# Both projections of an MLP on one core: 2x2 blocks with seven products in place of eight

## The chip, the cores and the metric

The kernel runs on one core of a Trainium2 chip. The metric is the device time of one execution in microseconds (us), lower is better. Three runs of the kernel before took 1946.54, 1942.43 and 1945.25 us (median 1945.25).

## What is computed

One inference step of a hybrid decoder layer: an input projection, dilated attention and a state-space branch, an output projection, and then the part that this change touches, a squared-ReLU MLP and the final norm. The prompt has 1024 tokens (1024 features each), the sample 8 tokens, and there are 4096 hidden features. All is float32.

```python
mix = jnp.concatenate([rms_norm(attn) * g_attn, y], axis=-1) @ w_out
x = x + g1 * mix
u = jnp.square(jax.nn.relu(modulate(x, sh2, sc2) @ w_up))     # (1024+8, 1024) @ (1024, 4096)
x = x + g2 * (u @ w_down)                                     # (1024+8, 4096) @ (4096, 1024)
y_prompt = rms_norm(xp) * g_final
```

## The kernel before, in words

Activations lie with the features on the 128 partitions and the tokens along the columns: `x1` is 8 blocks of 128 features by T = 1032 columns (1024 prompt, 8 sample), held in SBUF. A float32 product is made of three matmuls of the rounded type fp32r (`mm3`, L60 to L64): high part by high part, weight high by data low, weight low by data high. The high part is a copy on ACT (L51, for weights L442), the low part a subtract on DVE (L52, for weights L443). A matmul takes a 128x128 block of weights and one of the three column chunks of `NCH`: 352, 352 and 328 columns.

`phase_out` (L1479) is the output projection: 8 feature blocks by 3 chunks, each with 8 blocks of y and 8 of the attention. `gated` (L1402) adds a result, times its gate, into `x1` on DVE (L1406). Behind the groups of a chunk, `h2_stats` and `h2_cols` make the normed and modulated input of the MLP as a pair of tiles (high, low). The last chunk's runs on into the MLP.

`phase_mlp` (L1684) goes through 16 blocks of 256 hidden features: `up_block` of b+1, then `down_block` of b. An up group (one of 6 per block) is 8 k x 3 matmuls into a PSUM bank, then ReLU on ACT (L1723), square on DVE (L1724) and the split of the result (L51, L52). A down group (one of 24 per block) is 2 k x 3 matmuls and one `gated`. The weights come through `WStream`: raw loads of 1 MB, one ahead, split in pieces of 512 columns by `ws.step()`. Each `ws.get` issues two background copies (`background`, L54), which move the sample's key and value caches from DRAM to DRAM: 64 pieces of 512 rows, 2 MB each, all in the MLP.

Every one of these DMAs is issued by SP, in program order. Each engine executes its instructions in program order. `Side` is a generator that is advanced by estimated costs, so that norm work is written between the matmul groups. In the tail the last two blocks are taken in four column ranges, with the final norm of a finished range (`final_tiles`, L1773) beside the matmuls of the next.

Of the kernel before, what the change touches and what calls it, by code (L numbers as in the profile page):

```python
# [14 lines left out]
D = 1024  # L15
S = 1024
NB = 8
T = S + NB
KT = 8
NCH = ((0, 352), (352, 704), (704, 1032))  # L20
EPS = 1e-6
# [6 lines left out]
class Trunk:  # L28
# [364 lines left out]
    def mod_sample(self, pool, x, rb, blk, hi, lo):  # L393
# [5 lines left out]
        self.split(hi, lo, ts)  # L399
class WStream:  # L400
# [113 lines left out]
class InProj:  # L514
# [167 lines left out]
    def feat_gemm(self, acc, wt, col, consume):  # L682
        hi, lo = wt
        for a, b in NCH:
# [7 lines left out]
            consume(a, b, ps[:, :b - a])  # L692
            self.cw.step()
# [225 lines left out]
class Sample:  # L919
# [124 lines left out]
    def decode_scores(self, sb, sc, unit):  # L1044
# [3 lines left out]
        kv = lambda: sb.tile([128, D], F32, name="dkv", tag="dkv", bufs=6)  # L1048
# [352 lines left out]
class Rest:  # L1401
# [11 lines left out]
    def out_group(self, acc, w, x, m, n):  # L1413

        a, b = NCH[n]
# [3 lines left out]
        for k in range(KT):  # L1419
            self.mm3(ps[:, :W], whi[:, k], wlo[:, k], hi[:, k, :W], lo[:, k, :W], k == 0, k == KT - 1)  # L1420
            if k < KT - 1:
                yield 430
        self.gated(m, a, b, ps[:, :W], 2)
        yield 430

    def pair(self, n, c):

        a, b = NCH[n]
# [3 lines left out]
    def y_load(self):  # L1432

        i = self.y_n
        if i < self.y_end:
            self.y_n += 1
            a, e = NCH[i // 4][0], min(NCH[i // 4][1], S)
            k = 2 * (i % 4)
            yt = self.yt_pool.tile([128, 2, 352], F32, name="yt", tag="yt")
# [3 lines left out]
    def y_cols(self, n, cost):  # L1443

        a, b = NCH[n]
# [33 lines left out]
    def phase_out(self, eh, eo, ey, o_tok):  # L1479
# [4 lines left out]
        self.y_end, self.yt_pool = 12, self.pool(ey, "yt", bufs=4, side="right")  # L1484
        for _ in range(4):
            self.y_load()
# [8 lines left out]
        ys, aas, hs = self.ys, [], []  # L1495
        self.h2 = hs
# [23 lines left out]
        def attn_cols(n):  # L1520

            a, b = NCH[n]
# [20 lines left out]
        def h2_stats(sq, p, wait=5000):  # L1543

            yield wait
            for i in range(3):
                nc.tensor.matmul(p[:, i:i + 1], sq[:, 128 * i:128 * i + 128], self.ones[:, 0:1], start=True, stop=True)
            rs = self.sm.tile([128, 3], F32, name="r2", tag="r2", bufs=2)
            self.rstd(self.sm, rs, p[:, 0:3], [128, 3], "r2")
            yield 2500  # L1550
            for i in range(3):
                nc.tensor.transpose(p[:, 128 + 128 * i:256 + 128 * i], rs[:, i:i + 1].to_broadcast([128, 128]), self.ident)
            yield 500

        def h2_cols(n, p, cost=900):

            a, b = NCH[n]
            e, W = min(b, S), b - a
            r = p[:, 128:128 + W]
            hi, lo = pair(n, "h")  # L1560
            hs.append((hi, lo))
            if b > S:
                self.mod_sample(self.sm, self.x1[:, :, S:T], r[:, e - a:W], 3, hi[:, :, e - a:W], lo[:, :, e - a:W])
            ts = {}
            for k in range(KT + 1):
                if k < KT:
                    t = ts[k] = self.sm.tile([128, 352], F32, name="t2", tag="t2", bufs=3)
                    nc.vector.scalar_tensor_tensor(t[:, :e - a], self.x1[:, k, a:e], self.mod[:, 4, k, 0:1], r[:, :e - a],
                                                   op0=OP.mult, op1=OP.mult)
                    nc.scalar.activation(hi[:, k, :e - a], t[:, :e - a], AF.Identity, bias=self.mod[:, 3, k, 0:1], scale=1.0)  # L1570
                if k:
                    nc.vector.scalar_tensor_tensor(lo[:, k - 1, :e - a], ts[k - 1][:, :e - a], self.mod[:, 3, k - 1, 0:1],
                                                   f32(hi[:, k - 1, :e - a]), op0=OP.add, op1=OP.subtract)
                yield cost

        def first_w(wp):

            hi, lo = [self.up.tile([128, 2064], F32R, name="w0", tag="u", bufs=4)[:, 0:2048] for _ in range(2)]
            self.w0 = [t.rearrange("p (k n) -> p k n", k=KT) for t in (hi, lo)]
            raws = []  # L1580
            for i in range(2):
                raw = wp.tile([128, KT, 128], F32, name="ow_raw", tag="ow_raw", bufs=2).rearrange("p k n -> p (k n)")
# [481 lines left out]
```

## Time and profile before

| | |
|---|---|
| median of three runs | 1945.25 us |
| the profiled execution's own time | 1945.86 us |
| its span | 1944.1 us |
| mean granted clock of TensorE over the span | 0.987 |
| busy: PE, PEld, DVE, ACT, POOL | 1865.6, 1737.2, 1176.7, 670.5, 398.8 us |
| DMA: bytes, mean rate | 341.62 MB, 176 GB/s |
| MLP without tail and last part: 1198 to 1905 us | PE busy 706.03 of 707 us |

PE is the TensorE matmul, PEld its weight load, DVE the vector engine, ACT the scalar engine, POOL GpSimd, SP the engine that issues DMAs. A matmul's own duration in the records (0.32 us) overlaps the next one's, so the rate is read from the distance between starts. A DMA share over 1.00 is an overlap of the records likewise. The stretches that are named below are counted in us from the start of the span: input projections 165 to 520, attention and state-space work to about 950, output projection to 1198, MLP to 1944.

### The profile page before, as it was taken

The page shows a single profiled execution, that of the slowest core. Times are in us where ns is not written, and L with a number is a line of the kernel's source. Part 1 is how long each engine was busy: PE and PEld are TensorE (multiplying, and loading weights), DVE is VectorE, ACT ScalarE, POOL GpSimd, SP SyncE. Part 2 cuts the span into 40 slices and gives each one's busy share as a digit, 9 for nine tenths or more (in the row PEclk, how much of TensorE's full clock was granted, in tenths as well). Part 3 has the DMA queues.
Part 4 walks back from the last instruction along what each step waited for, and adds up shares of the span by engine and source line. Part 5 has one row for each costly group of instructions (what it writes and reads, how often), then busy time and mean ns, then how long its engine had stood idle before and what let it go on. Part 6 is the DMA issues. An engine that isn't in the chain of part 4 may idle for free.

```text
span 1944.1 us, 33819 instructions
## 1 busy us (share of the span) xinstructions
PE 1865.6 (96%) x13390; PEld 1737.2 (89%) x13390; DVE 1176.7 (61%) x2886; ACT 670.5 (34%) x1665; POOL 398.8 (21%) x382
## 2 busy tenths in 40 slices
PE   5899999999999989999899999999999999999998
PEld 3679999999999987766677899999999999999997
DVE  4613684857486796888834537655555555555566
ACT  3511434343521324877630324322222222222222
POOL 0011142434230462899400021000000000000000
PEclk8999999999999999999999999999999999999999
DMA  9673212132243766877365113656676656666665
GB/s 283 254 254 127 78 55 65 59 90 85 72 133 129 203 197 172 234 195 195 101 212 195 55 44 109 217 217 217 234 264 237 239 217 216 231 251 250 241 229 174
DMA packets 185546, 341.62 MB, mean 176 GB/s; under 512 B 27296, under 2 KB 152864, under 8 KB 180993
## 3 DMA queue, kind: packets, MB, share of 16 engines
q1 hardware_dynamic: 181804, 326.09, 50.8%
q0 software_dynamic: 3376, 13.30, 2.2%
q8 instruction: 105, 1.72, 0.4%
q14 instruction: 53, 0.43, 0.1%
q10 hardware_dynamic: 208, 0.07, 0.0%
HBM read 304.86 MB, written 168.85 MB: 244 GB/s over the span
## 4 chain that ended last, share of the span: by engine, by line
PE 78%; DVE 7%; POOL 5%; DMA 4%; ACT 2%; issue 2%; SPq 0%; DVEq 0%; POOLq 0%; ACTq 0%
PE acc L62 23%; PE acc L63 22%; PE acc L64 22%; POOL dkv L1082 2%; DMA aw<-in_w_ada 2%; POOL dkv L1086 1%; DVE ab L628 1%; PE y_ps L839 1%; PE y_ps L832 1%; DMA vw_raw<-in_w_in 1%; PE misc L1155 1%; DVE qw_lo L443 1%; PE s L1265 1%; PE o L1303 1%; PE pt L1287 1%
## 5 line engine op out<-in xcount | busy, mean ns | idle before, releaser
L1406 DVE SCALAR_TENSOR_TENSOR x<-acc,mod,x 128x352 f32<-128x352 f32 (+2 forms) x432 | 239.0, 561 | 148.3 <-PE acc L64 142.0
L62 PE MATMUL acc<-u,mw_hi 128*128 128x352 f32 (+3 forms) x800 | 251.7, 315 | 0.2 <-DVE gs L1410 0.2
L63 PE MATMUL acc<-u,mw_hi 128*128 128x352 f32 (+3 forms) x800 | 251.1, 314 | 0.0
L64 PE MATMUL acc<-u,mw_lo 128*128 128x352 f32 (+3 forms) x800 | 250.4, 313 | 0.0
L63 PE MATMUL acc<-h_lo,mw_hi 128*128 128x352 f32 (+1 forms) x720 | 230.3, 320 | 0.0
L62 PE MATMUL acc<-h_hi,mw_hi 128*128 128x352 f32 (+1 forms) x720 | 229.8, 319 | 0.0
L64 PE MATMUL acc<-h_hi,mw_lo 128*128 128x352 f32 (+1 forms) x720 | 229.6, 319 | 0.0
L62 PE MATMUL acc<-h_hi,cw_hi 128*128 128x352 f32 (+1 forms) x576 | 192.5, 334 | 1.1 <-ACT cw_hi L442 1.1
L63 PE MATMUL acc<-h_lo,cw_hi 128*128 128x352 f32 (+1 forms) x576 | 184.5, 320 | 0.0
L64 PE MATMUL acc<-h_hi,cw_lo 128*128 128x352 f32 (+1 forms) x576 | 184.2, 320 | 0.2 <-DVE cw_lo L443 0.2
L1723 ACT ACTIVATE ur<-acc 128x352 f32<-128x352 f32 (+1 forms) x96 | 43.9, 457 | 394.6 <-PE acc L64 394.5
L1724 DVE TENSOR_TENSOR ur<-ur 128x352 f32<-128x352 f32 (+1 forms) x96 | 49.6, 517 | 168.9 <-ACT ur L1723 168.9
L62 PEld LDWEIGHTS acc<-u,mw_hi 128*128 128x128 f32 x800 | 150.4, 188 | 0.9 <-PE acc L64 0.4
L64 PEld LDWEIGHTS acc<-u,mw_lo 128*128 128x128 f32 x800 | 150.6, 188 | 0.0
L62 PE MATMUL acc<-h_hi,qw_hi 128*128 128x256 f32 (+1 forms) x512 | 150.4, 294 | 0.0
L63 PEld LDWEIGHTS acc<-u,mw_hi 128*128 128x128 f32 x800 | 150.3, 188 | 0.0
L64 PE MATMUL acc<-h_hi,qw_lo 128*128 128x256 f32 (+1 forms) x512 | 145.7, 285 | 2.0 <-DVE qw_lo L443 2.0
L63 PE MATMUL acc<-h_lo,qw_hi 128*128 128x256 f32 (+1 forms) x512 | 145.9, 285 | 0.0
L63 PEld LDWEIGHTS acc<-h_lo,mw_hi 128*128 128x128 f32 x720 | 135.4, 188 | 0.0
L62 PEld LDWEIGHTS acc<-h_hi,mw_hi 128*128 128x128 f32 x720 | 135.3, 188 | 0.0
L64 PEld LDWEIGHTS acc<-h_hi,mw_lo 128*128 128x128 f32 x720 | 135.2, 188 | 0.0
L1280 ACT ACTIVATE P<-P,st 128x256 f32<-128x256 f32 (+1 forms) x256 | 118.4, 467 | 2.6 <-DVE st L1269 2.6
(424 smaller groups left out, 4343.0 us busy)
## 6 DMA issues: line engine op xcount, KB each, us to landing
aw<-in_w_ada SPq DMA_DIRECT2D x16, 1024.0 KB
mw_raw<-in_w_down SPq DMA_DIRECT2D x16, 1024.0 KB
out_k_win_sample<-in_cache_k_win SPq DMA_DIRECT2D x8, 2044.0 KB
out_v_win_sample<-in_cache_v_win SPq DMA_DIRECT2D x8, 2044.0 KB
mw_raw<-in_w_up SPq DMA_DIRECT2D x15, 1024.0 KB
cw_raw<-in_w_in SPq DMA_DIRECT2D x24, 512.0 KB
dkv<-in_cache_k_win SPq DMA_DIRECT2D x24, 512.0 KB
dkv<-in_cache_v_win SPq DMA_DIRECT2D x24, 512.0 KB
```

The costliest lines, as they stand in the source:

```text
L62: mm(ps, lhi, rhi, start=first, stop=False)
L63: mm(ps, lhi, rlo, start=False, stop=False)
L64: mm(ps, llo, rhi, start=False, stop=last)
L443: self.pend = lambda: self.K.nc.vector.tensor_tensor(lo, src, f32(hi), op=OP.subtract)
L628: nc.vector.tensor_tensor(r[:, 1, :W], r[:, 1, :W], ab[1][:, 0, :W], op=OP.add)
L832: nc.tensor.matmul(y[64 * a:64 * a + 64, 128 * j:128 * j + 128], xdt[:, h], G[:, h], start=True, stop=(c == 0))
L839: nc.tensor.matmul(y[:, 256:512], Bt, xw.rearrange("p h d -> p (h d)"), start=True, stop=True)
L1082: nc.gpsimd.tensor_tensor(pd, pd, qbs[b], op=OP.mult)
L1280: nc.scalar.activation(P, P, AF.Exp, bias=st[:, i + u, a, 0:1], scale=-1.0, accum_out=st[:, i + u, a, 1:2])
L1406: nc.vector.scalar_tensor_tensor(self.x1[:, m, a:e], ps[:, :e - a], self.mod[:, blk, m, 0:1], self.x1[:, m, a:e], op0=OP.mult, op1=OP.add)
L1723: nc.scalar.activation(r[:, :W], ps[:, :W], AF.Relu)
L1724: nc.vector.tensor_tensor(r[:, :W], r[:, :W], r[:, :W], op=OP.mult)
```

## The change

Matrices are cut in 2x2 blocks and multiplied with seven block products (Strassen's scheme in Winograd's form); the sums of blocks before and after the products are made on DVE and POOL.

- Up: 16 pairs (q) of 128-feature blocks; the 1024 inputs are halved, the 1024 prompt columns too. Seven products per pair (j = 0 to 6), each 4 k x 3 matmuls of 512 columns into one bank. The right operands ("hops") are made once: j = 0, 1 from the normed first half, j = 2 to 6 by `t_prep` with 8 DVE subtracts, 20 splits and 8 POOL subtracts. The weight operands are made for each pair: four POOL subtracts or adds, then a copy on ACT and a subtract on DVE (`split_op`) for each product, written at k = 1 of the product before it.
- What a product gives is combined by `evict` with the earlier ones; ReLU and square are both on ACT. Four more POOL instructions per pair make sums of the squared blocks for the down projection. Seven blocks of 256 KB per pair go to DRAM (`u_d`, 28 MB in all) and come back in the down stage.
- Down: pairs in four chunks (4, 4, 4 and 3 pairs); per chunk and j four feature blocks m, each n k x 3 matmuls of 512 columns. Per m one `step` is written: two DRAM loads, one weight operand, one split of a loaded block. Results of j = 1, 4, 6 are gated into `x1`, those of j = 0, 2, 5, 3 are summed over chunks. In the last chunk the sums are combined by a list (`later`) of 16 gates on DVE and 16 adds on POOL, five entries per m. The last pair is done plainly, in four ranges of 256 columns, with the final norm.
- Sample: its 8 columns go through separate matmuls, in up 16 of 128 columns per pair, in down 4 of 256 columns for each of 32 feature blocks, both with unsplit float32.
- Output projection: chunks of 512, 256 and 264 columns. `x1` is stored to DRAM (24 stores) and reloaded in the down stage; the normed columns of the second half are written over it.
- Background copies: 256 pieces of 128 rows; 72 of them are now issued in the input projections, 184 in the MLP. Fewer buffers: the decode's `dkv` 5 (was 6), `yt` 3 (was 4).

Matmuls of the MLP before: 768 groups of three chunks, 16 x 6 x 24 + 16 x 24 x 6 = 4608 in all. Now 16 x 7 x 12 = 1344 of 512 columns in up, 3 x 7 x 48 + 7 x 36 = 1260 in down, 192 of 256 columns for the last pair, and 384 small ones for the sample.

```diff
+OCH = ((0, 512), (512, 768), (768, 1032))
...
             consume(a, b, ps[:, :b - a])
+            self.background()
...
+        for q in range(16):                                    # up_prep
+            if q < 15:
+                load(q + 1)
...
+            self.sample_up(q, r1, r2)
+            s3 = self.S3.tile()
+            if q >= self.EARLY:
+                op((q, 0), a11)
+            g(s3, a11, a21, op=OP.subtract)
+            g(a11, a22, s3, op=OP.subtract)
+            if q >= self.EARLY:
+                yield (q, 0)
+                op((q, 1), a12)
+            g(a12, a12, a11, op=OP.subtract)
+            g(a21, a21, a22, op=OP.add)
+            if q >= self.EARLY:
+                yield (q, 1)
+            for j, a in ((2, a11), (3, a21), (4, a12), (5, s3), (6, a22)):
+                yield op((q, j), a)
...
+        for k in range(4):                                     # t_prep
+            v(b11[k], b12[k], b11[k], op=OP.subtract)
+            t2.append(self.UB.tile())
+            v(t2[k], b22[k], b11[k], op=OP.subtract)
+            self.split(*hops[2][k], t2[k])
+            yield
...
+            elif j == 4:                                       # evict, up
+                b = st[12, q] = self.UB.tile()
+                v(b, ps, st["t", q], op=OP.add)
+                square(b)
+                b11 = st.pop((11, q))
+                if q < 15:
+                    t1 = st["t1", q] = self.UB.tile()
+                    self.later += [lambda: g(t1, b, b11, op=OP.subtract), store(0, q, b11), store(3, q, t1)]
...
+                def hook(k):                                   # phase_up
+                    if k == 1:
+                        step()
+                        next(side, None)
+                    if k in (0, 2):
+                        self.pop_later(1 + len(self.later) // 8)
+                    if q == 0:
+                        next(side, None)
+
+                product(q, j, bank(), self.ops.pop((q, j)), hook)
+                if j:
+                    self.background()
...
+            if j == 5 and c == len(self.CHUNKS) - 1:           # evict, down
+                add = lambda o, a, b: lambda: nc.gpsimd.tensor_tensor(o[:, m], a[:, m], b[:, m], op=OP.add)
+                self.later += [lambda: gate(m, h0, P0[:, m]), add(U, U, P0),
+                               lambda: nc.sync.dma_start(P0[:, m], self.x1_d[:, m + 4, h1]),
+                               add(V3, V3, U), add(U, U, V5), lambda: gate(m, h1, V3[:, m]), add(V3, V3, V5),
+                               lambda: gate(m + 4, h0, U[:, m]), lambda: gate(m + 4, h1, V3[:, m])]
...
+                        if b == n:                             # phase_down
+                            if m < n or c + 1 < len(self.CHUNKS) and n < 4:
+                                step()
+                            evict(c, j, m, pss[m])
+                            self.pop_later(5)
+                            self.background()
...
-                for a in range(0, 2047, 512):
-                    e = min(a + 512, 2047)
+                for a in range(0, 2047, 128):
+                    e = min(a + 128, 2047)
```

Three places in the engines' order. The first is DVE at the start of the up stage. Before, three kinds of row alternate (square, low part of the result, low part of a weight):

```order
L1724 TENSOR_TENSOR ur<-ur 128x352
L52 TENSOR_TENSOR u<-ur,u 128x352
L443 TENSOR_TENSOR mw_lo<-mw_raw,mw_hi 128x512
```

Now, behind the norm of the last columns (`L1598`), the right operands of `t_prep` stand there (`L1883`, `L1885`, and `tl` from `L53`); `ol<-mr,oh` is the low part of a weight operand, `L1936` the first sum of two products:

```order
L1598 SCALAR_TENSOR_TENSOR t_13196<-x_10902,mod,misc 128x256
L1883 TENSOR_TENSOR x_10902<-x_10902 128x512
L1885 TENSOR_TENSOR ub<-x_10902 128x512
L53 TENSOR_TENSOR tl_13213<-ub,th_13212 128x512
...
L53 TENSOR_TENSOR tl_13215<-x_10902,th_13214 128x512 x4
L1936 TENSOR_TENSOR b_13272<-acc,p_13249 128x512
L53 TENSOR_TENSOR tl_13217<-x_10902,th_13216 128x512 x4
L53 TENSOR_TENSOR ol<-mr,oh 128x512
L53 TENSOR_TENSOR tl_13219<-x_10902,th_13218 128x512 x4
L1936 TENSOR_TENSOR b_13332<-acc,p_13301 128x512
L53 TENSOR_TENSOR ol<-mr,oh 128x512
```

The three rows `L1883`, `L1885`, `L53` come four times. So 8 subtracts and 12 splits stand ahead of the first `ol` shown, which the product (3, 1) needs, and four splits more ahead of the second, for (0, 2).

The second is ACT in the middle of the up stage. Before, each group has three rows:

```order
L1723 ACTIVATE ur<-acc 128x352
L51 CAST u<-ur 128x352
L442 CAST mw_hi<-mw_raw 128x512
```

Now one pair of feature blocks reads (`L1933` evicts the product j = 0, `L1923` is ReLU, `L1924` square, `L52` the high part of the weight operand of the product after next):

```order
L1933 COPY p_14364<-acc 128x512
L52 CAST oh<-mr 128x512
L1923 ACTIVATE ub<-ub 128x512
L1924 ACTIVATE ub<-ub 128x512
L52 CAST oh<-mr 128x512 x2
L52 CAST oh<-ms 128x512
L1923 ACTIVATE ub<-ub 128x512
L1924 ACTIVATE ub<-ub 128x512
L52 CAST oh<-mr 128x512
```

In the products that are squared, the high part of the weight operand of the product after next now stands behind ReLU and square of this one.

The third is DVE in the last chunk of the down stage. Now (`L2161` sums over chunks, `L2150` is a gate; U_16250, U_16251 and U_16252 are the summed products, `ol` and `bo` the low parts of weight and data):

```order
L2161 TENSOR_TENSOR U_16252<-acc,U_16252 128x512
L2150 SCALAR_TENSOR_TENSOR x_16256<-U_16250,mod,x_16256 128x512
L2150 SCALAR_TENSOR_TENSOR x_16256<-U_16251,mod,x_16256 128x512
L2150 SCALAR_TENSOR_TENSOR x_16256<-x_16256,mod 128x512
L53 TENSOR_TENSOR ol<-mr,oh 128x512
L53 TENSOR_TENSOR bo<-ub,bo 128x512
L2150 SCALAR_TENSOR_TENSOR x_16256<-acc,mod,x_16256 128x512
```

and POOL has there, four times over:

```order
L2163 TENSOR_TENSOR U_16250<-U_16250,x_16256 128x512
L2163 TENSOR_TENSOR U_16251<-U_16251,U_16250 128x512
L2163 TENSOR_TENSOR U_16250<-U_16250,U_16252 128x512
L2163 TENSOR_TENSOR U_16251<-U_16251,U_16252 128x512
```

Before, DVE had only `L1406` and `L443` at such a place, and POOL had nothing. Now three of four gates stand behind adds of POOL and ahead of the low parts of the next product.

## Rows read from the trace of the kernel before

**Rows 1.** Windows: input projections, two MLP stretches, tail.
```profile
core 0: us, PE busy (x) PEld busy (x) DVE busy (x) ACT busy (x) POOL busy (x), PEclk, DMA share, GB/s
...
165.00:520.00 355.00, 348.16 (x2431) 335.13 (x2429) 220.51 (x470) 141.75 (x261) 108.88 (x112) 1.00 0.25 70
...
1198.00:1905.00 707.00, 706.03 (x4535) 704.77 (x4533) 417.14 (x980) 167.26 (x340) 1.28 (x1) 1.00 0.65 236
1905.00:1944.00 39.00, 29.97 (x254) 29.38 (x254) 24.17 (x62) 10.14 (x32) 0.00 (x0) 0.94 0.37 136
```

**Rows 2.** Timeline of PE: start us, us, instruction; 352, 328 and 256 columns.
```profile
1215.63 0.31 PE L62 MATMUL acc<-h_hi,w 128*128 128x328 f32 x1
...
1219.23 0.31 PE L62 MATMUL acc<-h_hi,w 128*128 128x328 f32 x1
...
1500.76 0.33 PE L62 MATMUL acc<-h_hi,mw_hi 128*128 128x352 f32 x1
...
1507.54 0.32 PE L62 MATMUL acc<-h_hi,mw_hi 128*128 128x352 f32 x1
...
1913.26 0.28 PE L63 MATMUL acc<-u,mw_hi 128*128 128x256 f32 x1
...
1917.17 0.28 PE L63 MATMUL acc<-u,mw_hi 128*128 128x256 f32 x1
```

**Rows 3.** Lines, small float32 matmuls: duration ns min/median/max, first and last start us.
```profile
L119 PE MATMUL ada_acc<-aw,cT x128: 379/403/636, 20.5 to 50.8; 128*32 128x256 f32 x128
```

**Rows 4.** Timeline of PE and ACT in an up block, the releaser in brackets.
```profile
1238.31 0.31 PE L62 MATMUL acc<-h_hi,mw_hi 128*128 128x328 f32 x1
...
1238.57 0.47 ACT L1723 ACTIVATE ur<-acc 128x352 f32<-128x352 f32 x1 [1.80 <-PE acc L64]
```

**Rows 5.** Groups by line: count, busy us, mean ns, idle before, releaser.
```profile
L812 ACT ACTIVATE dec<-dec 128x512 f32<-128x512 f32 x32 | 20.2, 632 | 35.3 <-DVE dec L810 35.3
...
L442 ACT CAST mw_hi<-mw_raw 128x512 fp32r<-128x512 f32 x124 | 72.3, 617 | 62.9 <-DMA mw_raw<-in_w_up 42.8 <-DMA mw_raw<-in_w_down 20.1
...
L1406 DVE SCALAR_TENSOR_TENSOR x<-acc,mod,x 128x256 f32<-128x256 f32 x48 | 22.1, 479 | 10.4 <-PE acc L64 10.4
...
L1797 DVE SCALAR_TENSOR_TENSOR fo<-fp,frs,gb 128x512 f32<-128x512 f32 x16 | 11.2, 745 | 0.1
```

**Rows 6.** Lines of DVE and POOL: duration ns min/median/max, first and last start.
```profile
L443 DVE TENSOR_TENSOR mw_lo<-mw_raw,mw_hi x124: 681/684/691, 1211.8 to 1889.2; 128x512 fp32r<-128x512 f32 x124
...
L443 DVE TENSOR_TENSOR cw_lo<-cw_raw,cw_hi x48: 674/690/1770, 177.3 to 488.3; 128x512 fp32r<-128x512 f32 x48
...
L443 DVE TENSOR_TENSOR qw_lo<-qw_raw,qw_hi x32: 678/684/2891, 518.9 to 717.4; 128x512 fp32r<-128x512 f32 x32
...
L672 DVE TENSOR_TENSOR ab<-acc,rope_t x64: 674/692/708, 523.7 to 751.6; 128x512 f32<-128x512 f32 x48, 128x528 f32<-128x528 f32 x16
...
L813 POOL TENSOR_TENSOR dec<-dec,CB x32: 1280/1300/2552, 235.8 to 564.1; 128x512 f32<-128x512 f32 x32
```

**Rows 7.** Timeline of DVE and POOL at 538 us.
```profile
538.31 1.78 DVE L443 TENSOR_TENSOR qw_lo<-qw_raw,qw_hi 128x512 fp32r<-128x512 f32 x1
...
538.07 1.47 POOL L896 TENSOR_TENSOR sq<-sq 128x512 f32<-128x512 f32 x1
```

**Rows 8.** Windows of the MLP by DMA rate, and the highest sustained rate elsewhere.
```profile
40.00:50.00 10.00, 9.62 (x71) 8.28 (x67) 9.22 (x33) 5.51 (x14) 0.00 (x0) 1.00 1.04 409
...
1520.00:1524.00 4.00, 4.00 (x28) 4.00 (x27) 3.09 (x10) 2.18 (x4) 0.00 (x0) 1.00 1.61 615
...
1860.00:1900.00 40.00, 39.82 (x288) 39.14 (x287) 25.73 (x78) 10.06 (x21) 0.00 (x0) 1.00 0.90 324
```

More of the change, by code (lines that the diff above doesn't have):

```diff
@@ L1483, in phase_out @@
         self.mix = self.pool(eh, "mixp")
-        self.y_end, self.yt_pool = 12, self.pool(ey, "yt", bufs=4, side="right")
-        for _ in range(4):
+        self.y_end, self.yt_pool = 12, self.pool(ey, "yt", bufs=3, side="right")
+        for _ in range(3):
             self.y_load()
@@ L1566, in h2_cols @@
                 if k < KT:
[L1567 to L1573, printed above, removed]
+                    x, bias = self.x1[:, k, a:e], self.mod[:, 3, k, 0:1]
@@ new lines, in phase_out, with up_src, mul @@
+        return lambda p: chain(h2_stats(2, p, p[:, 128:], 4000), h2_cols(2, p[:, 128:], 600))
+    PAIRS = [(8 * c + i, 8 * c + 4 + i) for c in range(3) for i in range(4)] + [(24, 27), (25, 28), (26, 29), (30, 31)]
+    CHUNKS = (range(0, 4), range(4, 8), range(8, 12), range(12, 15))
+    EARLY = 4
+    DOWN = (0, 1, 2, 3, 5, 4, 6)
+    def up_src(self, f):
+        return self.I["w_up"][0].rearrange("(k p) n -> p k n", p=128)[:, :, 128 * f:128 * f + 128]
+    def mul(self, ps, w, b, first, last, hook=None):
+        n = len(w)
+        for k in range(n):
+            self.mm3(ps, *w[k], *b[k], first and k == 0, last and k == n - 1)
+            if hook:
+                hook(k)
@@ new lines, in pop_later, with phase_mlp, need, step @@
+    def pop_later(self, n=1):
+        while n and self.later:
+            self.later.pop(0)()
+            n -= 1
+    def phase_mlp(self, ex, es, eh, last_cols):
+        nc = self.nc
+        self.later = []
+        ew = ExitStack()
+        keep = self.pool(ew, "mk", side="right")
+        wp = self.pool(ew, "mw", side="right")
+        self.hs = keep.tile([128, KT, 32], F32, name="hs")
+        self.uS = keep.tile([128, 32, 32], F32, name="uS")
+        nc.gpsimd.memset(self.hs, 0.0)
+        nc.gpsimd.memset(self.uS, 0.0)
+        self.R, self.S3 = Rot([128, 1024], F32, "mr"), Rot([128, 512], F32, "ms")
+        self.OH, self.OL = [Rot([128, 512], F32R, t) for t in ("oh", "ol")]
+        self.UB = Rot([128, 512], F32, "ub")
+        for rot, n in ((self.R, 4), (self.S3, 1), (self.OH, 3), (self.OL, 3)):
+            rot.add(wp, n)
+        el = ExitStack()
+        prep = chain(self.up_prep(), self.down_prep())
+        done = set()
+        def need(key):
+            while key not in done:
+                done.add(next(prep))
+        def step(n=1):
+            for _ in range(n):
+                done.add(next(prep, None))
+        self.phase_up(ex, es, eh, el, ew, keep, last_cols, need, step)
+        self.phase_down(el, ew, need, step)
+        el.close()
+        ew.close()
@@ L1767, in phase_mlp @@
             if i < 3:
[L1768 to L1769 removed]
+                fin.start(chain((1300 for _ in range(1)), self.final_tiles(st, fps, gb, (a // 128, a // 128 + 1)),
+                                () if i else self.final_tiles(st, fps, gb, (8,))))
         for _ in last:
             pass
+        ep.close()
+        esm.close()
     def final_tiles(self, st, ps, gb, ts):
```

546 lines of the change are left out of this document (422 added, 124 removed).

## The prediction

> **What bounds the kernel now.** I read the stretches first: in the MLP from 1198 to 1905 us PE is busy 706.03 of 707 us [rows 1], so this part takes what its matmuls take, and a change in it is worth the PE time that it removes, less every wait that it puts in. DVE has 417 of these 707 us of work, ACT 167, POOL 1.3, the DMA engines a share of 0.65. None of them is waited for. The tail after 1905 us is 39 us, with PE at work for 30.
>
> The timeline of PE then gives the price of a matmul as the distance between starts [rows 2]: 328 columns 3.60 us / 24 = 0.150 us, 352 columns 6.78 / 42 = 0.1614, 256 columns 3.91 / 33 = 0.1185. The MLP before is 1536 matmuls of each chunk, so 1536 x (2 x 0.1614 + 0.150) = 726 us.
>
> **What the change removes: PE time.** No row has a matmul of 512 columns of this type. The line through 256 and 352 columns gives 0.1614 + 160 x 0.0429 / 96 = 0.2329, that through 256 and 328 gives 0.2305, and growth in proportion from 352 gives 0.2348. I take 0.2315, with ends 0.2275 (as far below as the highest is above) and 0.2348. Up 1344 x 0.2315 = 311.1, down 1260 x 0.2315 = 291.7, last pair 192 x 0.1185 = 22.8. The sample's matmuls go in fours to four strips of columns, as the float32 ones of 256 columns do that take 0.403 us each in the records [rows 3], started in fours. So 32 groups at 0.40 and 64 of half the width at about 0.20: 26 us. That is 651.6 us: **75 us less** (66 to 85). So 19% fewer columns in the split matmuls give 10%, since 7 of 8 is all that the scheme saves and the sample costs its own.
>
> The output projection has as many matmuls on as many columns in all, at the same price per column: nothing. Its 24 stores of x1 and the 72 background copies that move to the input projections find DMA at a share of 0.25 there [rows 1] beside a PE that is busy 348 of 355 us: nothing, and if the copies came in the way of weight loads, a few us. The smaller `dkv` and `yt` are loads in stages with DMA to spare; I price them at 0 (0 to 3).
>
> **What it adds: waits of PE.** The prices: ACT starts 0.26 us behind the start of the next group's first matmul [rows 4]; a 512-wide ACT pass takes 0.62, with 0.632 for an activation [rows 5]; a DVE subtract 0.685 and a DVE sum of a bank with SBUF 0.69 [rows 6]; a POOL instruction of that shape 1.30 [rows 6]. A product is 12 x 0.2315 = 2.78 us.
>
> 1. *Start of up.* The norm of the last 264 columns lies on DVE until some 20 us in (statistics, sample, 8 scalings). Behind it, in order, stand 8 subtracts and 12 splits, about 21 x 0.69 = 14.5 us, before the weight operand of (3, 1) is done, at about 35 us. PE has seven products before that, 19.5 us. So it stands for 15 us; then four splits, a sum that waits for product (3, 1), and POOL's two instructions with cast and subtract for (0, 2) cost another 9. **24 us** (15 to 30).
> 2. *Pairs 1 to 3*, still with right operands and sums late: **7** (4 to 10).
> 3. *Pairs 4 to 15.* After a squared product the chain is 0.26 + 0.69 (sum) + 0.62 (ReLU) + 0.62 (square) + 0.60 (high part of the operand after next, which stands behind the square on ACT) + 0.69 (low part) = 3.48 us. PE wants the low part with its third matmul, at 2.78 + 0.46 = 3.24. That is 0.24 late at each of four squared products, 1.0 us per pair, if nothing else meets it. But the subtract also meets POOL, which starts t1, b12 and t4 at the end of the same square. The rows show what that can cost: the subtract takes 681 to 691 ns in the MLP, where POOL is idle, and up to 1770 and 2891 in the two earlier stages where POOL works [rows 6]; at 538.31 us it took 1.78 beside a POOL instruction of 1.47 [rows 7]: 1.1 more. The medians there are still 690 and 684, so most were untouched. With one collision per pair at 1.1 us this is 12 x 2.1 = **25** (12 with none, 52 with three).
>
> The page "SBUF — State Buffer" of the Trainium skill, section "Who interferes with whom", says that a DVE instruction with two SBUF inputs and a GpSimd instruction that reads SBUF exclude each other for the whole instruction. The trace agrees in kind: L672, which reads PSUM, keeps its 674 to 708 ns beside POOL [rows 6]. By that rule every one of the three meetings per pair would wait, up to 1.30 us each: 12 x (1.0 + 3.9) = 59 in place of 25.
>
> 4. *Up to down:* the last square before the first operands, **3** (1 to 5).
> 5. *Chunk borders of down.* Inside a chunk each m has 12 matmuls, 2.78 us, with four pairs, against DVE's two subtracts and a sum, 2.07, and ACT's two casts, 1.24: hidden. At j = 1 and 2 POOL has two instructions per pair, 2.6 us, beside them; if port time adds, 1.4 + 2.6 = 4.0 against 2.78 for the 8 steps of a chunk. The buffers (nine operands) take most of it: **8** (3 to 14).
> 6. *Last chunk.* 16 gates with both inputs in SBUF (0.7 each) and 16 POOL adds (1.3) alternate, each waiting for the other, ahead of the low parts for j = 4, 6 and the last pair. POOL alone needs 16 x 1.3 = 21 us, with the gates it waits for 21 + 11 = 32, against 8 groups of 9 matmuls, 16.7 us. The difference is 15; I take **17** (4 to 24).
> 7. *Tail.* A range of 256 columns is now 48 x 0.1185 = 5.7 us, beside final-norm work of about 7.8 on DVE (8 gates at 0.48, two tiles at 2 x 0.745 [rows 5] and small work): **3** (0 to 6).
>
> Together 87 us (39 to 141). Against 75 saved, the sum is +12: the profiled execution's 1945.86 becomes 1958, and on the scale of the median, 0.61 lower, **1957 us**.
>
> What I cost at nothing: the 7 stores and up to 7 DRAM copies per pair in up. A pair moves 7 x 0.26 + 1.05 + 6 x 0.52 = 6.0 MB in 19.4 us, 311 GB/s; the trace shows 324 sustained with a share of 0.90, 409 early on, and 615 in short bursts [rows 8]. The cover is that rate; the stores wait for nothing that PE needs.
>
> **Rivals.**
>
> *The waits stay small* (faster, 0.40). The square chain overlaps (an operand has three buffers), the port is seldom met, and the last chunk's gates hide. For it: the medians of 684 and 690 in stages full of POOL work [rows 6]. Against: at the start and in the last chunk the order itself makes DVE late. With the low ends, 39 us, it gives -36: 1909; with 60, 1930. The point from which it decides is a total of 71 us of waits, that is the start and the pairs 4 to 15 together at 33 in place of 49.
>
> *Every meeting at the port costs a whole instruction* (slower, 0.08). Then term 3 is 59 in place of 25, and the time 1957 + 34 = 1991. For it: [rows 7]. Against: the medians.
>
> *The down stage is bound by DMA* (slower, 0.05). Per m it wants 0.26 (a block of u) + 0.15 (weights) + 0.52 (a background copy) = 0.94 MB in 2.78 us, 337 GB/s, more than the 324 that the trace holds over 40 us at a share of 0.90 [rows 8], until the copies run out: 96 of the 184 go in up, so 88 steps remain. At 300 GB/s those steps last 0.35 us longer each: +31 at most, half of it likely: 1957 + 16 = 1973. The copies are short-lived and u was just written; the loads are pumped ahead.
>
> *The saving and the waits cancel* (0.09): within 0.2%, 3.9 us either side, which is about what a measurement of this kernel can tell from no change. This needs waits of 71 to 79 us.
>
> **How the numbers follow.** My forecast, waits of 79 to 110 us, has 0.38 and its own range is 1949 to 1980. Faster 0.40, same 0.09, slower 0.38 + 0.08 + 0.05 = 0.51. So the forecast's sign and the other are almost level; the predicted time is that of the likeliest slower case, and not of the mean. The range, 1905 to 1990, takes in the small-waits case to its low end and the forecast with the DMA case; beyond lie the lowest waits with the cheapest matmul (1899) and the full port rule: some 0.15.
>
> **What would show it.** In the changed profile: starts of 512-column matmuls 0.228 to 0.235 us apart (else the 75 is wrong); PE's busy time in the MLP near 650 us; a hole of 15 us or more in PE some 20 us after the start of up, put down to DVE's `ol` or to `tl`; PE idle of about 2 us per pair behind DVE `ol`, with subtracts of up to 1.8 us beside POOL; a DMA share below 1 in the down stage, without PE waiting for `ub`; idle time of 10 us or more at the last chunk behind DVE or POOL. If PE waits under 70 us in all, the time is below that of before, and the terms 1, 3 and 6, in this order, are where I was wrong. If PE waits for `mr` or `ub` loads, the DMA case is the right one.

## The result, and the profile after

The change makes the kernel slower: 2005.54 us (median of 4 runs, 2003.90 to 2009.59) against 1944.82 us, a ratio of 1.0316 (95% interval 1.0297 to 1.0335), or 61 us. The forecast was slower, 1957 us, with a range up to 1990; the time lies 15.5 us above that range.

The page of the kernel after, its span and the busy time of each engine:

```profile
span 2003.4 us, 32735 instructions
...
PE 1836.5 (92%) x12252; PEld 1526.1 (76%) x12252; DVE 1221.8 (61%) x2533; ACT 802.2 (40%) x1875; POOL 711.3 (36%) x590
...
PEclk7999999999999899999999997899999989999988
```

PE has 29 us less to do than before (1865.6 us), and the span is 59 us longer. Windows of the kernel after (columns as in [rows 1]), from the end of the output projection on:

```profile
1198.00:1260.00 62.00, 37.39 (x196) 30.81 (x195) 41.80 (x79) 29.36 (x59) 19.44 (x15) 0.75 0.27 77
1260.00:1330.00 70.00, 59.33 (x327) 42.37 (x316) 37.39 (x44) 25.87 (x46) 38.97 (x28) 0.98 0.71 236
1330.00:1610.00 280.00, 265.45 (x1420) 196.22 (x1419) 130.99 (x179) 116.00 (x206) 133.10 (x97) 1.00 0.79 266
1610.00:1650.00 40.00, 32.31 (x154) 20.40 (x154) 25.01 (x25) 16.59 (x31) 22.81 (x15) 0.83 1.00 364
1650.00:1700.00 50.00, 50.00 (x222) 41.42 (x221) 28.21 (x44) 27.79 (x52) 1.67 (x1) 1.00 0.97 368
...
1900.00:1935.00 35.00, 29.55 (x136) 23.58 (x134) 32.05 (x38) 11.34 (x21) 15.66 (x10) 0.95 0.22 68
1935.00:1975.00 40.00, 31.39 (x188) 26.99 (x188) 32.16 (x60) 5.97 (x19) 8.28 (x5) 0.83 0.13 46
```

Where before PE was at work all the time from 1198 to 1905 us [rows 1], now it is so in the middle of the down stage alone: from 1650 to 1900, of which the rows show the first 50 us, at a DMA share of 0.97 and 368 GB/s, more than [rows 8] held over 40 us. A matmul of 512 columns, from the timeline of PE in that stretch:

```profile
1659.73 0.39 PE L63 MATMUL acc<-bo,oh 128*128 128x512 f32 x1
...
1662.45 0.39 PE L63 MATMUL acc<-bo,oh 128*128 128x512 f32 x1
```

These two are 12 matmuls apart: 2.72 / 12 = 0.227 us, a little under the lower end that the prediction set. So 2604 x 0.227 = 591 us of PE. The sample's matmuls take more than forecast: about 1.05 us per pair in up and 0.79 us per block in down (one m of a product with them starts 3.52 us behind the last, one without 2.73), 16 x 1.05 + 32 x 0.79 = 42 us. With the last pair that is 656 us against 726: 70 us less.

The sum of the 59 us, all from the two traces: the MLP begins at 1210.9 us, before at 1198.3: **+12.6**. PE's work: **-70**. The rest, **+117**, is PE's waiting and its work at the lower clock, with the longer tail; the records show 74 us of it as idle time of PE in the MLP (before: 1.8). Its parts are set beside the forecast's further below. The first of them, in the timelines of PE, DVE and POOL at the start of up:

```profile
1231.65 0.39 PE L65 MATMUL acc<-h_hi,ol 128*128 128x512 f32 x1
1253.64 0.79 PE L63 MATMUL acc<-h_hi,oh 128*128 128x512 f32 x1 [21.61 <-ACT oh L52]
...
1229.74 0.68 DVE L1883 TENSOR_TENSOR x<-x 128x512 f32<-128x512 f32 x1
...
1231.91 1.00 DVE L53 TENSOR_TENSOR tl<-ub,th 128x512 fp32r<-128x512 f32 x1 [0.69 <-ACT th L52]
...
1241.93 6.66 DVE L53 TENSOR_TENSOR tl<-x,th 128x512 fp32r<-128x512 f32 x4
1248.52 0.68 DVE L1936 TENSOR_TENSOR b<-acc,p 128x512 f32<-128x512 f32 x1
1251.06 2.50 DVE L53 TENSOR_TENSOR tl<-x,th 128x512 fp32r<-128x512 f32 x4 [1.87 <-ACT th L52]
...
1241.33 6.72 POOL L1897 TENSOR_TENSOR ub<-x,ub 128x512 f32<-128x512 f32 x4
```

DVE starts with the right operands at 1229.74, 19 us into the stage, and PE stands from 1232 to 1253.6. Four splits take 6.66 us beside four POOL instructions of 6.72, so 1.67 each in place of 0.69 [rows 6]; the next four, with POOL idle, take 2.50. DVE also waits for the high parts that ACT makes (0.69 us in each of the first four rounds, 1.87 ahead of 1251.06). Behind the hole the next product takes 5.3 us, twice the usual, with a granted clock of 0.50 from 1253.6 to 1258.9: the 1.2 GHz level.

And one pair in the middle of up (timelines of DVE, POOL and PE):

```profile
1540.12 1.38 DVE L53 TENSOR_TENSOR ol<-mr,oh 128x512 fp32r<-128x512 f32 x1 [1.87 <-ACT oh L52]
...
1539.66 1.29 POOL L1951 TENSOR_TENSOR ub<-ub 128x512 f32<-128x512 f32 x1 [8.93 <-ACT ub L1924]
...
1541.55 0.49 PE L65 MATMUL acc<-th,ol 128*128 128x512 f32 x1 [0.68 <-DVE ol L53]
```

The low part of a weight operand meets `t1` on POOL, takes twice its time, and PE's third matmul waits for it.

### The profile page after: what moved, and what is told of

The parts are those of the page before. It is cut to its first block, busy times and chain, and to the rows that moved or that the text cites. A ratio compares the mean times of both kernels' runs of the same rounds, so it can differ in the third digit from the quotient of the medians.

```text
span 2003.4 us, 32735 instructions
## 1 busy us (share of the span) xinstructions
PE 1836.5 (92%) x12252; PEld 1526.1 (76%) x12252; DVE 1221.8 (61%) x2533; ACT 802.2 (40%) x1875; POOL 711.3 (36%) x590
## 4 chain that ended last, share of the span: by engine, by line
PE 67%; DVE 11%; DMA 7%; ACT 6%; POOL 4%; issue 4%; SPq 1%; POOLq 0%; DVEq 0%; ACTq 0%
PE acc L65 18%; PE acc L63 18%; PE acc L64 17%; DVE ol L53 3%; PE s L1294 2%; PE o L1332 2%; PE pt L1316 2%; DMA aw<-in_w_ada 1%; ACT oh L52 1%; DMA q_d<-ab 1%; ACT ub L1923 1%; PE y_ps L868 1%; PE y_ps L861 1%; DMA dkv<-in_cache_v_win 1%; DMA vw_raw<-in_w_in 1%
## 5 line engine op out<-in xcount | busy, mean ns | idle before, releaser
L53 DVE TENSOR_TENSOR ol<-mr,oh 128x512 fp32r<-128x512 f32 x186 | 164.0, 882 | 128.3 <-ACT oh L52 127.3
L64 PE MATMUL acc<-bo,oh 128*128 128x512 f32 (+1 forms) x484 | 186.6, 385 | 15.1 <-DVE bo L53 15.1
L63 PE MATMUL acc<-bo,oh 128*128 128x512 f32 (+1 forms) x484 | 189.6, 392 | 8.8 <-DVE x L2150 6.6
L65 PE MATMUL acc<-bo,ol 128*128 128x512 f32 (+1 forms) x484 | 185.6, 384 | 0.0
L65 PE MATMUL acc<-th,ol 128*128 128x512 f32 x320 | 129.4, 404 | 14.8 <-DVE ol L53 14.7
L52 ACT CAST bo<-ub 128x512 fp32r<-128x512 f32 x109 | 67.5, 619 | 170.0 <-PE acc L65 150.4
L63 PE MATMUL acc<-th,oh 128*128 128x512 f32 x320 | 130.9, 409 | 4.1 <-ACT oh L52 4.1
L64 PE MATMUL acc<-tl,oh 128*128 128x512 f32 x320 | 125.6, 392 | 0.0
L63 PEld LDWEIGHTS acc<-bo,oh 128*128 128x128 f32 x484 | 93.7, 194 | 38.5 <-issue 14.0
L64 PEld LDWEIGHTS acc<-bo,oh 128*128 128x128 f32 x484 | 93.7, 194 | 33.9 <-DVE bo L53 18.0
L52 ACT CAST oh<-mr 128x512 fp32r<-128x512 f32 x186 | 112.9, 613 | 12.0 <-POOL mr L1826 5.9
L1923 ACT ACTIVATE ub<-ub 128x512 f32<-128x512 f32 x60 | 38.0, 633 | 192.0 <-DVE ub L1946 89.5
L53 DVE TENSOR_TENSOR bo<-ub,bo 128x512 fp32r<-128x512 f32 x109 | 105.7, 970 | 12.1 <-ACT bo L52 12.1
L63 PEld LDWEIGHTS acc<-h_hi,cw_hi 128*128 128x128 f32 x576 | 108.4, 188 | 2.1 <-ACT cw_hi L470 1.4
```

Source lines behind the costliest of these rows:

```text
L52: self.nc.scalar.copy(hi, src)
L53: (eng or self.nc.vector).tensor_tensor(lo, src, f32(hi), op=OP.subtract)
L63: mm(ps, lhi, rhi, start=first, stop=False)
L64: mm(ps, lhi, rlo, start=False, stop=False)
L65: mm(ps, llo, rhi, start=False, stop=last)
L1923: nc.scalar.activation(t, t, AF.Relu)
```

## The experiments

Theories: **A**, the weight operands of up are late (A1: the port of [rows 7]; A2: the chain over ReLU, square and cast); **B**, what lengthens the stages ahead of the MLP; **C**, the order on DVE at the start of up; **D**, the port there; **E**, DVE's work in the last chunk; **F**, PE's work for the sample; **G**, DMA at the start of down; **H**, the width of the sample's matmuls in down. All times are medians, beside 1943 to 1945 us of the kernel before, measured next to them.

**e1, operands two products ahead.** In the loop over the first products one more `step()` goes ahead (and one less is written at the end of up):

```diff
                 if q == self.EARLY - 1:
-                    step()
+                    step(1 + j)
```

> The weight operands of the up stage are written two products ahead in place of one; nothing else differs. Theory A (the low part of a weight operand is late, because its subtract shares a port with POOL or stands behind ReLU and square): in the changed kernel each pair from 4 on loses 2.9 us, of which two waits of 0.85 and 0.70 us are for such a subtract; two ahead hides both, and part of the 11 us of pairs 1 to 3. That is 12 x 1.5 + 3 to 6 = 21 to 24 us less, 1982 to 1985 us. Rival (the loss sits in PE's own short gaps or in DMA): under 5 us less, 2000 us or more.

1975.01 us, ratio 1.0153 (1.0138 to 1.0169): 30.5 us less, more than theory A said. The same window of the two kernels, the change first:

```profile
1340.00:1560.00 220.00, 208.27 (x1101) 153.85 (x1101) 102.70 (x138) 88.81 (x158) 106.10 (x77) 1.00 0.80 266
```
```profile
1340.00:1560.00 220.00, 219.05 (x1256) 176.72 (x1255) 117.42 (x154) 100.47 (x176) 121.23 (x85) 1.00 0.88 294
```

A pair takes 20.7 us in place of 23.0, and PE is busy 219 of 220 us. The DMA share rises, and PE hardly waits at all. So 2.3 of the 2.9 us lost per pair were lateness of the operands.

**e2, the result's sums on DVE.** `evict` of up: `v = g = nc.vector.tensor_tensor`.

> The four sums of squared blocks per pair (t1, b12, t2, t4) are made on DVE in place of POOL. Theory A1 (the port): the subtract beside them goes back from 1.38 to 0.69 us and the two waits per pair shrink, 12 x 1.0 to 1.5 = 12 to 18 us less, 1988 to 1994 us, though DVE gets 2.8 us more per pair (it is busy 47% of that stage). Theory A2 (the chain of ReLU, square and cast on ACT alone is what is late): no gain, 0 to 10 us more, 2005 to 2016 us.

1998.42 us (1.0278; 1.0262 to 1.0294), 7 us less, between the two expectations. A pair takes 22.3 us, 0.7 less. So taking these four instructions off POOL gives back a quarter of the loss per pair, net of the 2.8 us of work that DVE gets; the rest is A2, or POOL's four instructions on weights, which stayed.

**e3, copies in the output projection.** No `background()` in the input projections, three with each `attn_group`.

> The 72 background copies that the change issues in the input projections are issued in the output projection instead (three with each of 24 groups). Theory B (they are what makes the stages before the MLP 9 us longer): 517 to 761 us shrinks to 517 to 752 and the run by 9 us, less what they cost in the output projection (0 to 4): 1997 to 2001 us. Rival (the longer stretch comes from the smaller buffers or from where the data lie): no change, 2003 to 2008 us.

2035.69 us (1.0469; 1.0441 to 1.0498): 30 us more. Both halves of the expectation fell. The stretch that ends at 766 us there and at 761 in the change is no shorter without the copies, so they did not make it long. And in the output projection they cost 23 us; the chain of waits of ACT there:

```profile
ACT w L52 <- DMA ow_raw<-in_w_up: 24.4, 1, 24.4
```

The first weights of the MLP are queued behind 72 copies. ACT waits for them 24.4 us with the statistics behind that cast, and PE waits for the statistics. That the DMA engines had a share of 0.23 there in the change did not make the copies free.

**e4, the first weight operands ahead of the right operands.**

```diff
         side = self.t_prep(ex, el, hops, tp)
+        self.over = [fp.tile([128, 512], F32R, name=t, tag=t, bufs=1) for t in ("u2", "t")]
+        step()
...
-                if q == self.EARLY - 1:
+                if q + j == 2:
                     step()
```

> At the start of up the weight operand of (3, 1) is written ahead of the right operands (its two tiles borrow buffers that are idle then), and that of (0, 2) behind the first four of them. Theory C (PE's 22 us hole and the waits behind it come from the order on DVE, that is 8 subtracts and 12 splits ahead of that operand): the loss up to the end of pair 0, 34.6 us, falls to 17 to 24, so 10 to 17 us less, 1988 to 1995 us. Rival (the right operands themselves are late, whatever the order): 0 to 5 us less, 2000 us or more.

2006.28 us (1.0309; 1.0286 to 1.0331): no gain, as the rival said. PE's timeline, its two waits now:

```profile
1251.28 0.80 PE L63 MATMUL acc<-th,oh 128*128 128x512 f32 x1 [8.91 <-ACT oh L52]
...
1269.12 0.80 PE L63 MATMUL acc<-th,oh 128*128 128x512 f32 x1 [12.21 <-ACT oh L52]
```

The hole of 22 us became two of 9 and 12: what is ahead of one operand is then ahead of the next.

**f1 and f2, what lengthens the stages before.** f1 is the kernel before with `bufs=5` for `dkv`; f2, on top of e1, moves the lines of `x1_d` and `u_d` in `emit` behind those of the other DRAM tensors.

> The kernel before with five dkv buffers in place of six, nothing else. The stretch from 517 us to the start of attention is 9 to 15 us longer in every kernel with the change, also where the background copies were taken out of the input projections. Theory B1 (the buffers: another layout in SBUF or a load that waits for one makes it longer): 6 to 15 us more than before, 1951 to 1960 us. Rival B2 (it comes from the new DRAM tensors that lie ahead of the others): no change, 1942 to 1947 us.

> On top of the operands two ahead (1975 us): the two new DRAM tensors (x1_d, u_d, 32 MB) are allocated behind the old ones, so that q_d, k_d, bc_d and the rest lie where they lay before. Theory B2 (the place of those in DRAM makes the small transfers at 640 to 770 us slow): the start of the MLP comes back from 1211 to 1217 us to about 1200, so 9 to 15 us less, 1960 to 1966 us. Rival B1 (buffers) or B3 (neither): no change, 1972 to 1977 us.

f1: 1943.22 us, 1.0003 (0.9993 to 1.0013), nothing. f2: 1962.45 us, 12.6 less than e1, and the MLP starts at 1203 us. So it is the order in which the DRAM tensors are declared. Two more runs change it alone:

> The change with one thing undone: its two DRAM tensors lie behind the old ones. Theory B2: 11 to 14 us less than 2005 us, 1991 to 1994 us, the start of the MLP at about 1200 to 1204 us. Rival (it only helped beside the other edit): under 4 us less.

> The kernel before with the two DRAM tensors of the change declared ahead of its own (each gets one small store at the end, and nothing reads them). Theory B2: 9 to 14 us more than before, 1952 to 1958 us, all of it between 640 and 770 us. Rival (the place alone does nothing; something else of the change makes it matter): 1942 to 1948 us.

h2: 1990.69 us (1.0236; 1.0221 to 1.0252), 14.9 less than the change. h3: 1958.51 us, 1.0078 (1.0060 to 1.0095), 13.6 more than the kernel before, with nothing but two DRAM tensors declared ahead of the others. What SP waited for between 640 and 770 us, in the kernel before, h3, the change and f2:

```profile
SPq L989 <- DMA out_ssm_sample<-stS: 2.8, 1, 2.8
```
```profile
SPq L989 <- DMA out_ssm_sample<-stS: 17.2, 4, 6.4
```
```profile
SPq L1018 <- DMA out_ssm_sample<-stS: 14.6, 4, 6.0
```
```profile
SPq L1018 <- DMA out_ssm_sample<-stS: 4.7, 2, 2.9
```

Where the new tensors stand first, SP waits 14 to 17 us for the transfers of the sample's state, else 3 to 5. That this wait is what lengthens the stretch is argued from SP's order, not shown by a run of its own. Which tensor it is, and why its place matters, was not tried.

Not all of the change's late start is this. When the output projection begins (its first matmul with `ow_hi`), the change is 9.5 us late (975.3 for 965.8 us; h3 974.8). The other 3 us come in the output projection: it takes 235.6 us in place of 232.5 (238.5 in h2), and near its end PE waits for the statistics of its smaller chunks, where before it waited 1.1 us once (timeline of PE in the change):

```profile
1197.62 0.81 PE L1576 MATMUL otr<-ones,sq 128*128 128x1 f32 x4 [3.11 <-POOL sq L1670]
...
1205.39 0.66 PE L1581 MATMUL otr<-ident,r 128*128 128x128 f32 x2 [2.94 <-DVE r L78]
```

One profile can tell such parts to a few us only: among the versions with the new tensors declared last, the MLP starts between 1197 and 1204 us.

**f3, the right operands all on DVE**, on top of e1 (`v = g = nc.vector.tensor_tensor` in `t_prep`).

> On top of the operands two ahead (1975 us): the eight subtracts that POOL makes for the right operands are made on DVE. DVE gets 8 x 0.69 = 5.5 us more work at the start of up, where it is the engine that PE waits for. Theory D (POOL's eight instructions hold DVE's splits back to one per 1.7 us, 6.7 us for four): DVE's time falls by 8 x 1.0 and grows by 5.5, so 0 to 4 us less, 1971 to 1975 us, and four splits take 2.8 us. Rival (no lock; the splits are slow for another reason): 4 to 7 us more, 1979 to 1982 us, and splits as slow as before.

1972.65 us (1.0150; 1.0133 to 1.0167), 2.4 less and within the intervals, though the engine that PE waits for has 5.5 us more to do. The same four splits (timeline of DVE):

```profile
1245.14 2.50 DVE L53 TENSOR_TENSOR tl<-x,th 128x512 fp32r<-128x512 f32 x4 [0.31 <-ACT th L52]
```

2.50 us in place of 6.66: theory D. By the page "SBUF — State Buffer" of the Trainium skill, section "Who interferes with whom", a DVE instruction with two SBUF inputs contends with a GpSimd instruction that reads SBUF, for ports that one of them locks. Where both engines have several in a row, the trace of the change agrees: one DVE instruction per POOL instruction, and POOL's take 1.68 us where they took 1.30 [rows 6].

**f4, the short chunk second**, on top of e1: `CHUNKS` of 4, 3, 4, 4 pairs, and the count of steps per chunk to go with it.

> On top of the operands two ahead (1975 us): the chunk of three pairs in the down stage is the second in place of the last, so that the last chunk has four. Theory E (the 16 to 17 us that the last chunk loses is DVE's work, about 45 us with what the lock adds, against 16.3 us of PE in its last two products): j = 4 and 6 give PE 5.4 us more to do, so 4 to 6 us less, 1969 to 1971 us, and PE's waits there fall to about 11. Rival (the wait is a chain of POOL and DVE that has a length of its own, or the short chunk in the middle then stalls as well): 0 to 3 us either way, 1972 to 1978 us.

1973.89 us (1.0155; 1.0138 to 1.0172), 1.1 less: the rival. PE waits 10.9 us in the last chunk in four pieces, where it waited 12.3 in e1 (5.6, 2.4, 1.9 and 2.4 us); the longer products hid less than E said.

**g1 to g3, the start of up anew**, on top of e1 and f2. The core of the edit (g1 and g3 also have `v = g = nc.vector.tensor_tensor` in `t_prep`, as f3):

```diff
-    EARLY = 4
+    EARLY = 6
...
+        def early(k):
+            if k == 1 and q + j > 2:
+                step()
+            if k in (1, 3):
+                next(side, None)
...
             v(t2[k], b22[k], b11[k], op=OP.subtract)
-            self.split(*hops[2][k], t2[k])
-            yield
+            if k % 2:
+                yield
+        for k in range(4):
+            self.split(*hops[2][k], t2[k])
```

> On top of the two gains found (operands two ahead, new DRAM tensors behind the old ones, 1962 us): the start of up is written anew. Six pairs in place of four have their products 0 and 1 first, so PE has 12 products and not 8 before it needs a right operand; the right operands are all made on DVE, their eight first subtracts ahead of the splits, and spread over twice as many matmuls; the weight operands are two ahead here too. Theory C2 (DVE has about 36 x 0.62 = 22 us of right operands behind the norm, and PE needs matter that does not wait for them): the loss up to pair 0's end, 36 us, falls to 10 to 18, so 18 to 26 us less, 1936 to 1944 us. Rival (the hole only moves, as in e4, since DVE needs the same time for the same work): 0 to 8 us less, 1954 to 1962 us.

> As the run before it, but the second eight subtracts of the right operands on POOL, as the change has them. Theory D (the port): DVE has 5 us less to do and each of its splits beside POOL takes about 1 us more, eight of them, so 0 to 5 us more than the run before. Rival (no lock): 3 to 5 us less than it.

> As the first run of this call, with the chunks 4, 3, 4, 4 of the down stage (1 us in the run that had them) and the transposes of the output projection's statistics written two groups behind them in place of one, where PE waits 3 us for DVE twice. All that the theories promise together: 2 to 6 us less than the first run, and under the kernel before (1944 us) if that one is at 1944 or less.

g1: 1949.01 us (1.0024; 1.0014 to 1.0033), 13.4 less than f2, between the expectations: of the hole of 22 us a wait of 3.5 and one of 4.7 are left. g2: 1952.38 (1.0038; 1.0023 to 1.0053), 3.4 more than g1 with intervals that overlap: theory D, if any. g3: 1943.33 us, ratio 1.0001 (0.9989 to 1.0014): level with the kernel before, the best version found. Which of its two edits gave the last 6 us is not separated. The traces can't say, since the two profiled executions lie 1.4 us apart (1944.15 and 1942.73): in g3 PE waits 4.7 us for the statistics in one piece, in g1 3.1 and 1.9. The two versions below that have the chunks of g3 without its statistics, h1 and i1, lie near g1, but each has a further edit.

**g4, no sample in the MLP**, on top of e1 and f2.

> On top of the two gains (1962 us): the sample's matmuls in the MLP are left out, with what copies and combines them, so the sample's rows of y hold the input of the MLP alone. The trace has them at 1.05 us per pair in up and 0.79 us for each of 32 blocks in down, 17 + 25 = 42 us of PE. Theory F (PE is the bound there, so the sample apart costs what PE spends on it): 35 to 43 us less, 1919 to 1927 us. Rival (PE's time for it lies in holes that would be there anyway): under 20 us less, 1942 us or more. The prediction had 26 us for it.

1926.08 us (0.9902; 0.9886 to 0.9919), 36.4 less than f2, whose ratio is 1.0098 (1.0080 to 1.0115). The sample apart costs about 36 us of time, of 42 us of PE. Before, its 8 columns were part of the last chunk: 1536 x 8 x 0.447 ns, 5.5 us at the price per column between 256 and 352 in [rows 2].

**h4, the change without background copies** (the kernel leaves them out).

> The change without any background copy (the sample's cache outputs are left out, 64 MB read and 64 MB written less... each byte once read and once written). Theory (DMA bounds only the start of the down stage, and the rest of what was lost is DVE's, POOL's and the port's): 6 to 14 us less than 2005 us, 1991 to 1999 us. Rival (the up and down stages are bound by DMA, as the prediction's third case had it): 30 us less or more, 1975 us or under.

2001.95 us (1.0296; 1.0279 to 1.0314), 3.6 less, on intervals that overlap: DMA bounds little of the change. Where it does is the start of down, at a DMA share of 1.00 in the change (1610 to 1650 above): from its first matmul to the 101st of 512 columns it takes 40.1 us there and 34.4 in h4. The MLP starts at 1211.0 us in h4, so it is not the copies that delay it.

**h1, the copies kept from the start of down**, in the version of g3 with the statistics as they were.

> On top of the new start of up, the operands two ahead, the tensors behind and the chunks 4, 3, 4, 4 (but with the statistics as the change has them): no background copy is issued in the last two pairs of up or with the first two products of down; they follow later, where DMA has room. In the run at 1943 us the first operands of down wait for loads of u and of weights until 1571 us, at a DMA share of 0.99, and PE waits 11 us there. Theory G (those loads are behind copies): 4 to 9 us less than 1943 us, 1934 to 1939 us, under the kernel before. Rival (the loads of u wait for the stores of the last pair, or DVE's 1.76 us subtracts beside POOL hold PE there): 0 to 2 us less, 1941 to 1944 us.

1949.31 us (1.0026; 1.0011 to 1.0041): a miss. The same 101 matmuls take 38.2 us, in g3 38.6, so putting the copies off did not take these waits away; the DMA share is 1.01 to 1.05 there from 1560 to 1580 us all the same. And the copies put off now run on behind the last matmul, 14 us to the end in place of 10. The same version with its copies in place was not run, so the 6 us above g3 can't be put down to them alone.

**i1 and i2, the sample's matmuls of down in 128 columns**, in two banks.

> All that helped together: operands two ahead, tensors behind, the new start of up with the right operands on DVE, chunks 4, 3, 4, 4 (the statistics as the change has them, copies not deferred), and the sample's matmuls of the down stage in eight of 128 columns in two banks in place of four of 256 in one. Theory H (a group of four of 128 columns takes 0.26 us, so a block 0.52 in place of 0.79): 32 x 0.27 = 8.6 us less than the 1941 to 1943 us of this version without it, 1932 to 1936 us, faster than the kernel before by 0.4 to 0.6%. Rival (the width does not matter; a bank fewer for the products costs): 1941 to 1946 us, level.

> The same edit of the sample's matmuls alone, on top of the operands two ahead and the tensors behind (1962 us). Theory H: 6 to 9 us less, 1953 to 1956 us, and 3.25 us from one feature block to the next where it was 3.52. Rival: 1960 to 1966 us and 3.5 us.

i2: 1959.77 us (1.0082; 1.0057 to 1.0107) against 1962.45, on intervals that overlap; i1: 1947.65 us (1.0015; 1.0002 to 1.0028). Theory H fell: one m with the sample starts 3.56 us behind the last, and with 256 columns it was 3.52. The full version is not faster than the kernel before.

## Why the prediction was wrong, point by point

The sign was right, and so was the shape, a saving of PE and a larger sum of waits; the time was 48 us too low. The sign does not hang on what was missed: with the DRAM tensors put behind (h2), the change is still 46 us slower. Waits of PE in us, forecast and measured in the profiled execution (the column adds up to 62; less the 3 us of waits that the kernel before has in its own MLP, that is the 59):

| step | forecast | measured | what the runs showed |
|---|---|---|---|
| stages before the MLP | 0 | 12.6 | some 9.5 the place of the DRAM tensors (h2, h3), 3 the output projection |
| PE's work | -75 | -70 | matmul 0.227 for 0.2315; sample 42 for 26 |
| 1 start of up | 24 | 34.6 | 26.3 to the end of (3, 1), 8.3 in pair 0 |
| 2 pairs 1 to 3 | 7 | 11.3 | |
| 3 pairs 4 to 15 | 25 | 35 | 2.9 per pair; e1 takes away 2.3 |
| 4, 5 into down, chunk borders | 11 | 12.4 | all in the first chunk, none at the borders |
| 6 last chunk | 17 | 16.5 | |
| 7 tail | 3 | 10 | waits of 0.9 to 2.2 us where a range ends; clock 0.59 from 1955 to 1960 |

The longest wait of the last chunk (timeline of PE), and the window with the low clock:

```profile
1934.88 0.79 PE L64 MATMUL acc<-bo,oh 128*128 128x512 f32 x1 [5.45 <-DVE bo L53]
```
```profile
1955.00:1960.00 5.00, 5.00 (x29) 5.00 (x28) 2.45 (x7) 0.00 (x0) 0.00 (x0) 0.59 0.00 0
```

- **The step that failed most clearly** is the one costed at nothing: "The output projection ... nothing", with 0 to 3 us for the smaller buffers. The list of what the change touches ahead of the MLP had the copies, the stores and the buffers, and not the two new DRAM tensors. What was priced costs little (f1: the buffers of `dkv`, nothing; the output projection itself 3 us in the profiled execution, for waits on its statistics); what was not on the list costs 13.6 to 14.9 us (h3, h2). In h2 the change takes 1990.7 us, level with the upper end of the range, so this term carried the time out of the range; the terms below had used up the rest of it.
- **Term 1** had the mechanism and the size too low. It counted 21 instructions at 0.69 us, 14.5 us in all; from 1229.7 DVE takes 24.6 us to the end of that operand. Of the 10 us more, about 5 are the port, which the prediction weighed in the terms 3 and 5 and left out here (four splits at 1.67 beside POOL, others at 1.00; in f3 all take 0.69), and 4.6 are DVE's waits for ACT's high parts, which the sum had at nothing. It also left out the half clock behind the hole.
- **Term 3** had 25 us with ends of 12 and 52; 35 lies within. One collision per pair was taken, and the trace has two, of 0.7 us each. That it is lateness of one operand is shown by e1, that taking the four sums off POOL gives back a quarter of it, net, by e2. The share of the chain alone stays open.
- **The sample** was priced from one record of 0.403 us for a group of four; each block's matmuls come twice in the trace, 8 records for the 4 in the program, and a group costs 0.79 us (3.52 less 2.73).
- **Term 5** was wrong the other way: the chunk borders, with nine operand tiles, cost nothing, though POOL works beside them; that the nine tiles are the reason was not tried.
- **Term 6** held (16.5 for 17). **The DMA rival** fell for the stage as a whole: 368 GB/s at a share of 0.97 without a wait of PE, and 3.6 us less without the copies. It holds for the first 40 us of down, where the copies cost 5.7 us of PE's time (h4). **The other side** (faster) would have needed 71 us of waits, and there were 120, where the kernel before had 3. **The full port rule** as a price for term 3 (59) was too high.
- **Slips of the working:** a lower end of the matmul's price "as far below as the highest is above" is 0.2282 and not 0.2275, and the split matmuls have 13% fewer columns and not 19%. Neither moves the forecast.

## What to carry to other kernels

A scheme that saves an eighth of the products saves less on PE once the parts that don't fit it go separately (here 70 of 726 us, with 36 us for 8 columns), and each sum it makes on DVE or POOL must be early by more than one product: one step of lead was worth 30 us here. Price what a change declares as well as what it executes: two DRAM tensors ahead of the others were worth some 14 us, ahead of the stages that use them, and moving their lines back undid it. Where DVE and POOL both read SBUF in long rows, count one of POOL's instructions for each of DVE's (1.67 us for 0.69 here).

## What the runs showed of the hardware

- The order in which DRAM tensors are declared changed the time: 1944.9 to 1958.5 us in h3, with no other work added than two small stores at the end, and SP's waiting for the transfers of the sample's state went from 2.8 to 17.2 us.
- POOL and DVE in a row, with two inputs each from SBUF, take turns: four DVE splits in 6.66 us beside four POOL instructions, 2.50 us without them.
- DMA held 368 GB/s over 50 us with PE busy all the time.
- Behind a wait of 22 us PE's next product ran at the 1.2 GHz level (granted clock 0.50, 5.3 us for 2.72), so this hole cost 2.6 us more than its own length.
